# A tenth Strassen pair in the input projection: two merge-gate tiles join it, and the keys' pair moves to its end

## The chip, the cores and the metric

The kernel runs on one core of one Trainium2 chip. The time is what one execution takes on the device, in microseconds; the median of three runs stands for a kernel. A core has five engines that run side by side and wait for each other by semaphores: TensorE (PE, matmuls), VectorE (DVE), ScalarE (ACT), GpSimd (POOL) and SyncE (SP, which here issues the loads). PE writes to PSUM, in banks of 512 fp32 columns; DVE and ACT move results from there to SBUF.

## The reference

One residual block with two token mixers and a SwiGLU, for 512 tokens of width 1024. What matters here is the combined input projection (h, the normalized x, times w_in, its columns split by `IN_SPLITS`) and the GLA mixer that runs beside it (4 heads, chunks of 64):

```python
IN_SPLITS = (GLA_QK_W, GLA_QK_W, GLA_V_W, GLA_V_W, GLA_GATE_RANK,
             NSA_Q_W, NSA_KV_W, NSA_KV_W, NSA_KV_W, NSA_KV_W, NSA_KV_W, NSA_KV_W,
             NSA_GATE_W, D_MODEL, D_MODEL)
...
    attn = jnp.where(causal, jnp.einsum('bhncd,bhnsd->bhncs', qe, ke), 0.0)
    o = jnp.einsum('bhncs,bhnse->bhnce', attn, vh)
...
    o = o + jnp.einsum('bhncd,nbhde->bhnce', qe, s_prev)
    o = o * lax.rsqrt(jnp.mean(o * o, axis=-1, keepdims=True) + RMS_EPS) * norm_g.astype(jnp.float32)
...
    return (o * jax.nn.silu(r.astype(jnp.float32))).astype(r.dtype)
```

GLA's output is A, that of the other mixer (NSA: compressed, selected and window attention, 8 heads) is B, and the two meet as sigmoid(gA) * (A @ w_proj_gla) + sigmoid(gB) * (B @ w_proj_nsa). The last two parts of the split, 1024 columns each, are the merge gates gA and gB. The two parts of 128 columns that are keys of the selected and the window branch are "the keys" below.

## The kernel before, in words

Everything is transposed: a tile is 128 output columns (on the partitions) by 512 tokens. Tiles of the input projection are numbered; `T_GK`, `T_GQ` are GLA's keys and queries, `T_R` its output gate, `T_NQ` NSA's queries, `T_KV` the compressed branch's two inputs and, from `T_KV + 2`, the keys, `T_MA` and `T_MB` the merge gates. Every big fp32 matmul is done as three fp32r products (`three`, L243, L248, L249): high by high, low by high and high by low part. So a weight tile needs a cast (`whi`, ACT L78) and a difference (`wlo`, DVE L85, or an accumulating DMA from POOL).

A **plain** tile takes 8 blocks x 3 matmuls of 512 columns. A **pair** is two tiles computed together by Strassen's scheme in Winograd's form (`EPAIRS`, `eproduct`): 7 products, in the order a11, s2, s3, s1, a22, s4, a12 (`USE`), each of 4 x 3 matmuls of 256 columns. Each product has its weight form: sums of blocks of the two tiles (`esums`, `esum_s1`, `esum_s4`, on DVE) that are split into high and low (`eform`: L415 cast on ACT, L351 difference on DVE, or L418 on ACT and a DMA L420 on POOL). The results go out half by half: a11 by an ACT copy (L490), s2, s3, s1, a22 and s4 by DVE adds (L487), a12 by an ACT copy (L506). A pair has two PSUM banks, and successive pairs take them in opposite order (`ebank`). Where a form lies is fixed by `eplace`: the a22 form of every pair but the last lies in the places tagged `kst` + "s" or "w" (`eks`, `ekw`), that of the last in `e1`, `e2` (`fe`); s4 and a12 forms are called `feq`. Where the results go is fixed by `early_dest`; the keys' tiles go into `kst` + "s"/"w" (`ksts`, `kstw`). The pair's sum `ex` lies in the place tagged `causal`, into which later the attention's mask is set (POOL memset and DMA, L890, L891).

Stages: projection of the token-major part (to about 76 us); then the stage of the pairs, in which GLA runs beside them (to about 229 us); then the compressed branch, attention and the rest. In the second stage `weave` mixes two lists: the products of the pairs and the remaining plain tiles (`Pieces`, `qa`) with the 19 steps of GLA (`gla_attn`, `gla_prep`, `gla_state`, `gla_out`, `gla_end` for four heads). `gla_out` squares its output on ACT (L726, four), forms the inverse root (DVE L287, POOL L288, `grs`) and scales (ACT L731, four); `gla_end` transposes (PE L739), multiplies (DVE L741) and splits (`gh` L273, `gl` L274). The order on each engine is then set by a scheduler that goes by its own estimates; on the chip each engine runs its list in that order.

The plain tiles come through a stream, `st`, that makes each tile's cast and difference one tile ahead. During the pairs this is held back (`st.limit`). At position 18 (`st.reset`) the weights' ring is opened anew: that tile's raw is fetched beforehand, but its cast can only come after the tile ahead has been handed out. Positions 16 to 19 are MA0 to MA3, 20 and 21 the compressed branch's KV0 and KV1. A merge-gate tile ends with a tanh on ACT (`merge_gate`, L771).

## Time and profile before

| | us |
|---|---|
| median of 3 runs (838.72 to 840.14) | 839.0 |
| the profiled execution | 838.92 |
| its span | 837.1 |
| TensorE busy | 823.3 |
| VectorE busy | 634.6 |
| ScalarE busy | 523.0 |
| GpSimd busy | 144.8 |

A row of the timeline has the start in us, the duration, engine, line, operation, output and inputs; in brackets how long the engine had been idle and what released it. A matmul's duration there is modelled and overlaps the next one, so what it costs in a stream is read from the distance between starts. A row of the groups (by line) has the count, the busy time, the mean in ns, and the idle time ahead with its releasers. A row of waits has the waiting engine and tile, the engine, tile and line waited for, the sum in us, how often, and the longest. A row of windows has, for a stretch, its length, then busy us and number of instructions of PE, weight loads, DVE, ACT and POOL, then the granted clock, the DMAs' share and GB/s.

### The profile page before, as it was taken

The page shows a single profiled execution, that of the slowest core. Times are in us where ns is not written, and L with a number is a line of the kernel's source. Part 1 is how long each engine was busy: PE and PEld are TensorE (multiplying, and loading weights), DVE is VectorE, ACT ScalarE, POOL GpSimd, SP SyncE. Part 2 cuts the span into 40 slices and gives each one's busy share as a digit, 9 for nine tenths or more (in the row PEclk, how much of TensorE's full clock was granted, in tenths as well). Part 3 has the DMA queues.
Part 4 walks back from the last instruction along what each step waited for, and adds up shares of the span by engine and source line. Part 5 has one row for each costly group of instructions (what it writes and reads, how often), then busy time and mean ns, then how long its engine had stood idle before and what let it go on. Part 6 is the DMA issues. An engine that isn't in the chain of part 4 may idle for free.

```text
span 837.1 us, 14656 instructions
## 1 busy us (share of the span) xinstructions
PE 823.3 (98%) x5561; PEld 751.2 (90%) x5561; DVE 634.6 (76%) x1205; ACT 523.0 (62%) x967; POOL 144.8 (17%) x174
## 2 busy tenths in 40 slices
PE   9999999999999999999999999999999999999995
PEld 8998899998787887888888999999999999889995
DVE  7765897883477878777666478998888778839986
ACT  6557767773544988887635587766665667445441
POOL 0101022230040000100000265111211110001353
PEclk9999999999999999999999999999999999999998
DMA  8434465762252444454327758778878883325333
GB/s 288 107 106 110 116 124 125 167 146 79 76 184 51 105 122 101 101 120 108 76 76 274 229 141 237 144 208 235 187 194 196 200 177 87 99 67 177 88 102 101
DMA packets 41238, 117.84 MB, mean 141 GB/s; under 512 B 4716, under 2 KB 7036, under 8 KB 41040
## 3 DMA queue, kind: packets, MB, share of 16 engines
q1 hardware_dynamic: 27952, 82.49, 31.3%
q0 software_dynamic: 12496, 33.88, 21.8%
q8 instruction: 43, 0.70, 0.4%
q10 hardware_dynamic: 720, 0.54, 0.2%
q14 instruction: 27, 0.22, 0.1%
HBM read 102.21 MB, written 4.19 MB: 127 GB/s over the span
## 4 chain that ended last, share of the span: by engine, by line
PE 90%; DVE 4%; ACT 4%; issue 1%; DMA 1%; POOL 0%; SPq 0%; DVEq 0%; ACTq 0%
PE ps_mm L243 13%; PE ps_mm L248 13%; PE ps_mm L249 13%; PE ps_sc L243 5%; PE ps_sc L249 5%; PE ps_sc L248 5%; PE ps_acc L243 4%; PE ps_acc L248 4%; PE ps_acc L249 4%; PE ps_tp L568 2%; PE ps_tp L249 2%; PE ps_tp L248 2%; PE ps_tp L243 2%; PE ps_sc L568 2%; PE ps_tp L1132 2%; PE ps_acc L568 1%
## 5 line engine op out<-in xcount | busy, mean ns | idle before, releaser
L78 ACT CAST whi<-wraw 128x1024 fp32r<-128x1024 f32 (+2 forms) x62 | 60.1, 973 | 67.3 <-PE ps_mm L248 25.5
L243 PE MATMUL ps_mm<-hT_hi,whi 128*128 128x512 f32 (+1 forms) x260 | 100.8, 388 | 0.2 <-ACT whi L78 0.2
L249 PE MATMUL ps_mm<-hT_hi,wlo 128*128 128x512 f32 (+1 forms) x260 | 97.4, 375 | 0.0
L248 PE MATMUL ps_mm<-hT_lo,whi 128*128 128x512 f32 (+1 forms) x259 | 96.8, 374 | 0.0
L85 DVE TENSOR_TENSOR wlo<-wraw,whi 128x1024 fp32r<-128x1024 f32 (+2 forms) x47 | 51.4, 1096 | 26.9 <-ACT whi L78 26.9
L243 PEld LDWEIGHTS ps_mm<-hT_hi,whi 128*128 128x128 f32 x260 | 49.0, 189 | 9.7 <-ACT whi L78 0.9
L249 PEld LDWEIGHTS ps_mm<-hT_hi,wlo 128*128 128x128 f32 x260 | 48.9, 188 | 9.3 <-DVE wlo L85 0.3
L248 PEld LDWEIGHTS ps_mm<-hT_lo,whi 128*128 128x128 f32 x259 | 48.8, 189 | 7.1
L1455 ACT CAST d_two<-s 128x1024 fp32r<-128x1024 f32 x26 | 27.0, 1044 | 30.5 <-PE ps_mm L249 15.0
L274 DVE TENSOR_TENSOR pl<-ps_tp,ph 128x512 fp32r<-128x512 f32 (+1 forms) x64 | 31.2, 490 | 19.1 <-ACT ph L273 18.6
L1093 ACT ACTIVATE p<-p,mx 128x512 f32<-128x512 f32 (+1 forms) x64 | 35.8, 561 | 6.7 <-DVE mx L1091 6.5
L1462 DVE TENSOR_TENSOR d_two<-s,d_two 128x1024 fp32r<-128x1024 f32 x25 | 30.6, 1224 | 11.2 <-ACT d_two L1455 10.9
L82 POOL DMA_DIRECT2D wlo<-wraw x15 | 12.8, 851 | 148.3 <-ACT wlo L81 80.6
L1091 DVE CUSTOM_DVE_ANT_0 p<-ps_sc,causal 128x512 f32<-128x512 f32 (+1 forms) x64 | 29.2, 486 | 6.5 <-PE ps_sc L1084 6.2
L273 ACT CAST ph<-ps_tp 128x512 fp32r<-128x512 f32 (+1 forms) x64 | 26.4, 414 | 4.0 <-PE ps_tp L1132 3.5
L1828 POOL TENSOR_TENSOR y<-y,us 128x256 f32<-128x256 f32 x12 | 15.2, 1293 | 72.3 <-DVE us L1825 72.2
L1132 PE MATMUL ps_tp<-ident,p 128*128 128x128 f32 x160 | 27.7, 272 | 0.0
L1132 PEld LDWEIGHTS ps_tp<-ident,p 128*128 128x128 f32 x160 | 20.7, 140 | 7.2 <-ACT pc L1022 0.4
L1439 POOL DMA_DIRECT2D wlo<-in_w_gate x13 | 11.5, 884 | 76.8 <-ACT wlo L1437 76.7
L1455 ACT CAST c_two<-s 128x1024 fp32r<-128x1024 f32 x12 | 12.5, 1045 | 18.8 <-PE ps_mm L249 7.0
L243 PE MATMUL ps_mm<-hT_hi,d_two 128*128 128x256 f32 x80 | 22.4, 281 | 0.0
L249 PE MATMUL ps_mm<-hT_hi,d_two 128*128 128x256 f32 x80 | 22.3, 279 | 0.0
(821 smaller groups left out, 3223.8 us busy)
## 6 DMA issues: line engine op xcount, KB each, us to landing
wraw<-in_w_t SPq DMA_DIRECT2D x36, 512.0 KB, 3.8
wraw<-in_w_gate SPq DMA_DIRECT2D x21, 512.0 KB, 4.4
rw<-in_w_up SPq DMA_DIRECT2D x19, 512.0 KB, 8.3
wlo<-wraw POOLq DMA_DIRECT2D x15, 512.0 KB, 4.5
wlo<-in_w_gate POOLq DMA_DIRECT2D x13, 512.0 KB, 8.6
w_uu<-in_w_up POOLq DMA_DIRECT2D x19, 256.0 KB, 8.7
wraw<-in_w_tok SPq DMA_DIRECT2D x11, 440.0 KB, 3.5
wraw<-in_w_proj SPq DMA_DIRECT2D x8, 512.0 KB, 3.5
```

Source lines behind the costliest of these rows:

```text
L78: self.cast = self.nc.scalar.copy(hi[:, :cols], raw[:, :cols])
L85: self.nc.vector.tensor_tensor(out=lo[:, :cols], in0=raw[:, :cols], in1=hi[:, :cols].bitcast(F32), op=OP.subtract)
L243: pe.matmul(o, wh, xh, start=start, stop=False, skip_group_check=True)
L248: pe.matmul(o[:, c], wh, xl[:, c], start=False, stop=False, skip_group_check=True)
L249: return pe.matmul(o, wl, xh, start=False, stop=stop, skip_group_check=True)
L274: dve.tensor_tensor(out=lo, in0=src, in1=hi.bitcast(F32), op=OP.subtract)
L568: pe.matmul(o, x[:, k, t], y[:, w], start=(k == 0 and m == 0), stop=(k == KD - 1 and m == 2))
L1091: dve.tensor_tensor_reduce(out=o, in0=s, in1=causal[:, S - n:S], scale=-1.0, scalar=-NEG, op0=OP.add, op1=OP.min, accum_out=mx[:, i:i + 1])
L1093: act.activation(out=o, in_=o, func=AF.Exp, scale=-1.0, bias=mx[:, i:i + 1], accum_out=z[:, i:i + 1])
L1132: pe.transpose(tp[:, i * 128:(i + 1) * 128], p[:, OFF[i] + k * 128:OFF[i] + (k + 1) * 128], ident)
L1455: act.copy(hi, t)
L1462: dve.tensor_tensor(out=lo, in0=t, in1=hi.bitcast(F32), op=OP.subtract)
```

## The change

The list of pairs has a tenth entry: MA0 and MA1 (`T_MA`), between the two later output-gate pairs; the query pairs stand together; the keys' pair is the last. So `with_gla` loses two tiles and the weave 8 fills of two. MA0's and MA1's results go to `two0` and `two1` in SBUF, and two tanh behind the weave read them from there. Space for this: the squares of the first stage go to base tags, the triangle mask to the tag `th`, there is one `at` instead of two, and `bl[2]`, `bl[3]` share the places `two0`, `two1`.

```diff
-    with_gla = [("h", n) for n in (T_GK, T_GQ, T_GK + 2, T_GQ + 2)] + [("h", T_MA + n) for n in range(4)]
+    with_gla = [("h", n) for n in (T_GK, T_GQ, T_GK + 2, T_GQ + 2)] + [("h", T_MA + n) for n in (2, 3)]
...
-            sq = acc_x if k == 0 else xin.tile([128, S], F32, tag="sqx", bufs=2, name="sqx")
+            sq = acc_x if k == 0 else base.tile([128, S], F32, tag=("b1", "b5")[k % 2], name="sqx")
...
-    EPAIRS += [(n, n + 1) for n in (T_R, T_R + 2, T_NQ, T_R + 4, T_NQ + 2, T_KV + 2, T_R + 6)]
+    EPAIRS += [(n, n + 1) for n in (T_R, T_R + 2, T_NQ, T_NQ + 2, T_R + 4, T_MA, T_R + 6, T_KV + 2)]
...
     def early_dest(n):
+        if n >= T_MA:
+            ta[n - T_MA] = mid.tile([128, S], F32, tag="two%d" % (n - T_MA), name="two%d" % (n - T_MA))
+            return ta[n - T_MA]
...
-    triu = param("triu", [128, 128], gt)
+    triu = gt.tile([128, S], F32, tag="th", name="triu")[:, 0:128]
+    pool.dma_start(triu, I["triu"])
...
-    ats = []
-    for i in range(2):
-        t = gt.tile([128, NT, 128], F32, name="at%d" % i)
-        pool.memset(t, 0.0)
-        ats.append(t)
+    at = gt.tile([128, NT, 128], F32, name="at")
+    pool.memset(at, 0.0)
...
-    weave(main + [lambda: qa.fill(2)] * 16, steps)
+    weave(main + [lambda: qa.fill(2)] * 8, steps)
+    tas[0] = mid.tile([128, 2, S], F32, tag="gh0", name="ta0")
+    for i in range(2):
+        ta[i] = merge_gate(T_MA + i, tas[0][:, i, :], ta[i])
...
-            bl[j] = mid2.tile([128, S], F32R, name="bl%d" % j)
+            bl[j] = (mid2.tile([128, S], F32R, name="bl%d" % j) if j < 2 else
+                     mid.tile([128, S], F32R, tag="two%d" % (j - 2), name="bl%d" % j))
```

`st.limit` and `st.reset` stay at 14 and 18. Position 18 of the stream was MA2 and is KV0 now. What that does to the engines' lists is shown at three places; a row is line, operation, output, inputs, size and what it waits for.

**First, DVE where the eighth pair's results of s1, a22 and s4 are added.** Before, this is the keys' pair:

```order
L351 TENSOR_TENSOR wlo<-wraw,whi 128x512 [waits PE_49,Activation_49]
L487 TENSOR_TENSOR kstw<-ps_mm,eus 128x256 [waits DMASW5_49,DMASW3_49,DMASW6_49,DMASW0_49,PE_49]
L351 TENSOR_TENSOR wlo<-ex,whi 128x512 [waits DMASW5_49,Activation_49]
L487 TENSOR_TENSOR kstw<-ps_mm,eus 128x256
L351 TENSOR_TENSOR wlo<-wraw,whi 128x512 [waits Activation_49]
L351 TENSOR_TENSOR ex<-wraw,ex 128x512 [waits DVE_49]
L487 TENSOR_TENSOR ksts<-ps_mm,eus 128x256 [waits PE_49]
```

In the change the eighth pair is MA0 and MA1 (an output-gate pair and the keys' pair follow):

```order
L351 TENSOR_TENSOR ex<-wraw 128x512 [waits DVE_49]
L487 TENSOR_TENSOR two_2064<-ps_mm,eus 128x256 [waits PE_49]
L438 TENSOR_TENSOR wraw<-wraw,ex 128x512 [waits DVE_49,Activation_49]
L351 TENSOR_TENSOR wlo<-ex,whi 128x512 [waits DMASW5_49,Activation_49]
L487 TENSOR_TENSOR two_2064<-ps_mm,eus 128x256 [waits PE_49]
L351 TENSOR_TENSOR wlo<-wraw,whi 128x512
L487 TENSOR_TENSOR two_2063<-ps_mm,eus 128x256 [waits PE_49]
```

The first add waited for four DMAs' and PE's use of its place; the add into `two` waits for its product alone.

**Second, ACT and POOL at the third head's output.** ACT before, from that head's squares to the copy of the last pair's a12 result (`sr`), behind which come the plain tiles' casts and tanh:

```order
L726 ACTIVATE go,gssq<-ps_acc 128x256 [waits PE_49] x4
L731 ACTIVATE go<-ps_acc,grs 128x256 [waits Activation_49,Pool_49]
L731 ACTIVATE go<-ps_acc,grs 128x256 [waits Activation_49]
L731 ACTIVATE go<-ps_acc,grs 128x256
L731 ACTIVATE go<-ps_acc,grs 128x256 [waits Activation_49]
L506 COPY sr<-ps_mm 128x256 [waits DVE_49,PE_49]
L764 ACTIVATE th<-sr 128x512 [waits DVE_49,Activation_49]
```

ACT in the change, where `sr` is the result of the pair ahead of the last one, and the last one's forms (`feq`) stand around it:

```order
L726 ACTIVATE go,gssq<-ps_acc 128x256 [waits PE_49] x2
L415 CAST feq_2316<-ex 128x512 [waits DVE_49,Activation_49]
L726 ACTIVATE go,gssq<-ps_acc 128x256 [waits PE_49] x2
L731 ACTIVATE go<-ps_acc,grs 128x256 [waits Activation_49,Pool_49]
L731 ACTIVATE go<-ps_acc,grs 128x256 [waits Activation_49]
L731 ACTIVATE go<-ps_acc,grs 128x256
L731 ACTIVATE go<-ps_acc,grs 128x256 [waits Activation_49]
L506 COPY sr<-ps_mm 128x256 [waits PE_49]
L415 CAST feq_2310<-wraw 128x512
```

POOL in the change; before, the memset, the DMA of `feq` and that of the mask stand in the pair ahead of that output:

```order
L893 MEMSET causal 128x512 [waits DVE_49]
L894 DMA causal<-in_tril_neg 128x128 [waits Pool_49]
L288 TENSOR_TENSOR grs<-grs,mhalf 128x4 [waits DVE_49]
L420 DMA feq_2311<-in_w_t 128x512 [waits DMASW3_49,PE_49,Activation_49]
L288 TENSOR_TENSOR grs<-grs,mhalf 128x4 [waits DVE_49]
```

The copy of `sr` stands behind the scalings in both; in the change the last pair's products follow it on PE instead of MA0 and MA1, and the mask's memset and DMA stand right ahead of the power that the scalings wait for.

**Third, PE and ACT at the end of the stage,** where the last merge-gate tile MA3 ends and KV0 begins. PE before:

```order
L739 MATMUL ps_tp<-ident,go 128x128 [waits PE_49]
L739 MATMUL ps_tp<-ident,go 128x128 x3
L243 MATMUL ps_mm<-hT_hi,whi 128x512
L248 MATMUL ps_mm<-hT_lo,whi 128x512
L249 MATMUL ps_mm<-hT_hi,wlo 128x512 [waits DVE_49]
```

PE in the change, where the third matmul is KV1's first and the fourth is KV0's again, followed by ACT from MA3's tanh on:

```order
L739 MATMUL ps_tp<-ident,go 128x128 [waits PE_49]
L739 MATMUL ps_tp<-ident,go 128x128 x3
L243 MATMUL ps_mm<-hT_hi,whi 128x512 [waits Activation_49]
L248 MATMUL ps_mm<-hT_lo,whi 128x512
L243 MATMUL ps_mm<-hT_hi,whi 128x512 [waits Activation_49]
L249 MATMUL ps_mm<-hT_hi,wlo 128x512 [waits DVE_49]
```
```order
L771 ACTIVATE ta_2493<-ps_mm 128x512 [waits PE_49]
L78 CAST whi<-wraw 128x1024 [waits DMAHW4_49]
L273 CAST gh<-sr 128x512 [waits DVE_49]
L78 CAST whi<-wraw 128x1024 [waits DMAHW5_49,DMASW4_49]
L273 CAST gh<-sr 128x512 [waits DVE_49]
```

Both tiles' casts now stand behind MA3's tanh, with one split of `gh` between them, where before KV0's first matmul waited for nothing.

More of the change, by code (lines that the diff above doesn't have):

```diff
@@ L687, in gla_attn @@
         q3, qk, ku, dec = gst[h]
-        at = ats[h % 2]
         ps = bank("tp")
@@ L716, in gla_out @@
         q3, qk, ku, dec, kut, ss = gst[h]
-        at = ats[h % 2]
         ps = [bank("acc"), bank("acc")]
```

## The prediction

> **What bounds the kernel now.** I read the page first: the busy shares and the chain of work that ended last.
>
> ```profile
> span 837.1 us, 14656 instructions
> PE 823.3 (98%) x5561; PEld 751.2 (90%) x5561; DVE 634.6 (76%) x1205; ACT 523.0 (62%) x967; POOL 144.8 (17%) x174
> ...
> PE 90%; DVE 4%; ACT 4%; issue 1%; DMA 1%; POOL 0%; SPq 0%; DVEq 0%; ACTq 0%
> ```
>
> PE is the bound nearly everywhere, so the change is worth the PE columns that it removes, plus the PE waits that it removes, less those that it adds. Next I asked for PE's waits between 76 and 230 us, which is the stretch that the change reorders.
>
> ```profile
> PE ps_mm L243 <- DVE kstw L487: 0.5, 1, 0.5
> PE ps_mm L243 <- DVE qst L487: 0.2, 1, 0.2
> PE ps_mm L243 <- ACT whi L78: 0.2, 1, 0.2
> ```
>
> There are three waits, each met once, and together they list under one microsecond. So what is there to win is small, and one new wait of a microsecond weighs as much as the columns saved.
>
> **1. Columns.** Two plain tiles are 2 x 24 matmuls of 512 columns. The pair that replaces them is 7 products x 12 matmuls of 256. From PE's timeline:
>
> ```profile
> 98.99 0.39 PE L248 MATMUL ps_mm<-hT_lo,whi 128*128 128x512 f32 x1
> ...
> 100.15 0.28 PE L243 MATMUL ps_mm<-hT_hi,whi 128*128 128x256 f32 x1
> ```
> ```profile
> 101.57 0.28 PE L243 MATMUL ps_mm<-et2gh,whi 128*128 128x256 f32 x1
> ...
> 101.92 0.28 PE L243 MATMUL ps_mm<-et2gh,whi 128*128 128x256 f32 x1
> ```
>
> The first column is the start, the second a modelled duration; what a matmul costs in a stream is the distance between starts. Five of 512 lie between 98.99 and 100.15, so 0.232 us each; three of 256 between 101.57 and 101.92, so 0.1167 us each. 48 x 0.232 = 11.14, 84 x 0.1167 = 9.80: **-1.34 us**. The half-wide matmul costs half, with nothing on top for its weight load.
>
> The Trainium skill, page "TensorE: Matmul & The Clock Gate", section "Back-to-back issue gap", says otherwise: in a sustained stream 128 columns take about 81 ns and 512 about 131, so a matmul's price falls far less than its width. On a line between the two, 256 columns would take some 98 ns (an estimate from that page), and the pair would cost 84 x 0.098 - 48 x 0.131 = +1.9 us where the rows give -1.34. The trace does not agree: its two widths stand at 1 to 2.
>
> **2. The wait on kstw.** This is the s4 product of the keys' pair.
>
> ```profile
> 181.68 0.38 PE L243 MATMUL ps_mm<-hT_hi,feq 128*128 128x256 f32 x1 [0.55 <-DVE kstw L487]
> 181.90 0.28 PE L248 MATMUL ps_mm<-hT_lo,feq 128*128 128x256 f32 x1
> ...
> 182.58 0.28 PE L248 MATMUL ps_mm<-hT_lo,feq 128*128 128x256 f32 x1
> ```
>
> The product accumulates where the pair's s1 result lies, and so waits for the add that moves that result into `kstw`. But this place still holds the pair's own a22 form (`ekw`), so the add waits until PE has done the a22 product, and PE then stands until the add is through. With the keys' pair last, its a22 form lies in `e1`/`e2`, and the eighth pair, now MA0 and MA1, writes to `two0`/`two1`, which nobody reads. The wait goes: 0.55 idle, and 0.22 to the next start instead of 0.11: **-0.65**. If it stayed, 0.
>
> **3. The wait on qst.**
>
> ```profile
> 145.00 0.28 PE L249 MATMUL ps_mm<-hT_hi,feq 128*128 128x256 f32 x1
> 145.50 0.39 PE L243 MATMUL ps_mm<-hT_hi,feq 128*128 128x256 f32 x1 [0.22 <-DVE qst L487]
> ```
>
> 0.50 between starts instead of 0.12: the a12 product of the first query pair waits for the add of its a22 result. In the changed order this add stands on DVE ahead of the `wlo` difference and the masked copy that it stood behind: **-0.38**, or 0 if DVE is late anyway.
>
> **4. The wait at the reset.** Position 18 of the stream is the tile whose raw is fetched but whose cast is not made ahead. Before, that is MA2.
>
> ```profile
> 212.26 1.02 PE L707 MATMUL ps_sc<-tok,gkut 128*128 128x256 f32 x4
> 212.46 0.60 ACT L771 ACTIVATE ta<-ps_mm 128x512 f32<-128x512 f32 x1 [1.18 <-PE ps_mm L249]
> ...
> 212.95 1.98 ACT L78 CAST whi<-wraw 128x1024 fp32r<-128x1024 f32 x2
> 213.12 1.03 PE L723 MATMUL ps_acc<-tok,at 128*128 128x256 f32 x4
> ...
> 214.04 0.50 PE L243 MATMUL ps_mm<-hT_hi,whi 128*128 128x512 f32 x1
> ...
> 214.38 0.40 PE L248 MATMUL ps_mm<-hT_lo,whi 128*128 128x512 f32 x1
> ...
> 214.99 0.51 PE L243 MATMUL ps_mm<-hT_hi,whi 128*128 128x512 f32 x1 [0.21 <-ACT whi L78]
> ```
>
> MA1 ends at 212.26 (call it T). The casts stand on ACT behind its tanh, and the first matmul of MA2 starts at T + 1.78. But eight GLA matmuls (L707, L723) fill 212.26 to 213.98, so only 0.06 is lost ahead of 214.04, then 0.34 - 0.23 = 0.11 and 0.61 - 0.23 = 0.38: **-0.55** when it goes.
>
> **5. New wait B: the same reset, now at KV0.** `with_gla` is two tiles shorter, so position 18 is now the first compress tile. What covers PE between the last merge-gate tile and KV0 is less:
>
> ```profile
> 228.40 1.03 PE L739 MATMUL ps_tp<-ident,go 128*128 128x128 f32 x8
> 229.19 0.48 PE L243 MATMUL ps_mm<-hT_hi,whi 128*128 128x512 f32 x1
> ```
> ```profile
> 228.45 1.06 ACT L78 CAST whi<-wraw 128x1024 fp32r<-128x1024 f32 x1
> ...
> 229.88 1.23 ACT L273 CAST gh<-sr 128x512 fp32r<-128x512 f32 x2
> ```
>
> Eight transposes, 0.79 us; before, KV0 follows them at once, since its cast had been made. After, ACT's order is tanh, KV0's cast, one split of `gh`, KV1's cast; so KV0 starts at T + 1.78 instead of T + 0.79: +0.99. Then PE's order has two matmuls of KV0 (0.34 + 0.23 by part 4) and, third, the first of KV1, which would stand at T + 2.35. KV1's cast waits for KV0's (from T + 0.69, 0.95 by the two starts in part 4) and for the split (1.23 / 2 = 0.61), ends 1.05 later at T + 3.3: +0.95. Everything of KV0 that could have run meanwhile is queued behind that matmul. **+1.95**; at the least 0.99 (only the first half binds), at the most 2.2 (a difference on DVE, L85, is late as well).
>
> **6. New wait A: the s2 product of the last pair.** Pairs take their two banks in alternating order, so the second product (s2) of the keys' pair writes the bank that the last result (a12) of the pair ahead is copied from, by ACT at L506. Before, two plain tiles came next there, and these needed the bank later.
>
> ```profile
> 194.51 1.02 PE L723 MATMUL ps_acc<-tok,at 128*128 128x256 f32 x4
> ...
> 197.35 0.48 PE L243 MATMUL ps_mm<-hT_hi,feq 128*128 128x256 f32 x1
> ```
> ```profile
> 198.31 0.17 DVE L287 TENSOR_SCALAR grs<-gssq 128x4 f32<-128x4 f32 x1 [3.17 <-ACT go L726]
> 198.57 1.03 POOL L288 TENSOR_TENSOR grs<-grs,mhalf 128x4 f32<-128x4 f32 x1 [10.78 <-DVE grs L287]
> 199.64 1.57 ACT L731 ACTIVATE go<-ps_acc,grs 128x256 f32<-128x256 f32 x4 [1.43 <-POOL grs L288]
> 201.08 0.39 ACT L506 COPY sr<-ps_mm 128x256 f32<-128x256 f32 x1
> ```
> ```profile
> 185.41 0.53 POOL L890 MEMSET causal<- 128x512 f32 x1 [6.62 <-DVE feq L351]
> 186.37 0.86 POOL L420 DMA_DIRECT2D feq<-in_w_t  x1 [0.43 <-ACT feq L418]
> 186.90 0.89 POOL L891 DMA_DIRECT2D causal<-in_tril_neg  x1
> ```
>
> Call the start of the third head's output P (194.51). PE does it in 2.84 (to 197.35), then a12 and the next a11 (24 x 0.1167 = 2.80) and one two-pass matmul (0.22): s2 is wanted at P + 5.86. The copy stands on ACT behind four squares, POOL's power and four scalings; at the old pace it ends at P + 6.57 + 0.39 = P + 6.96, which is 1.1 late. But on POOL the power now also stands behind the mask's memset and its DMA. The memset waits for the last pair's s4 difference on DVE (`feq`), which by the order comes behind the second square, at an estimated P + 3.35; with 0.53 and 0.89 the power starts at P + 4.77 and the copy ends at P + 7.8 (1.03 + 1.44 + 0.39 and gaps), 1.9 late. If the DMA holds POOL only for the 0.53 between 186.37 and 186.90, it is 1.5 late. Between these two: **+1.7**, ends 1.1 and 1.9. Behind s2 on PE stand the rest of the pair and everything later, so nothing fills the gap.
>
> **7. At nothing.** The squares' other places and the mask's tag free space and lie in the token stage, whose PE order is unchanged; one memset less is off the path. One `at` instead of two: the masked copy of head h + 1 must follow the output of head h, which PE's order has already. The two tanh of the pair read SBUF and have until the merge. Its three low parts come by accumulating DMAs from POOL, 0.86 each in the row at 186.37, on an engine that is 17% busy.
>
> **Sum.** -1.34 - 0.65 - 0.38 - 0.55 + 1.95 + 1.7 = +0.73. The profiled execution took 838.92 (its span 837.1 and 1.8 around), 0.08 below the median of 839.0: 838.92 + 0.73 + 0.08 = **839.7**.
>
> **A spread that no order tells.** 256 columns take 0.1167 at 101.57, but six of them from 181.90 to 182.58 take 0.113, 3% less. The matmuls run at one or the other pace for long stretches, and a wait can flip them. Of some 100 us reordered, if half changed pace: +-1.5, an estimate.
>
> **Rivals.**
> - **The waits A and B are covered** (PE comes later to both places, by waits elsewhere that take no more time in sum). Then -2.92: 836.1; with A at 1.1 alone, 837.2. For it: PE's present waits are tiny although the order is as tight in many places. Against: in both places the copy and the cast are queued behind something that is itself later than PE's need, by the rows above.
> - **DVE becomes the bound** between 170 and 190 us; this ends slower. A pair costs DVE eight 512-wide sums or differences and five adds of results, less the two `wlo` of plain tiles.
>
> ```profile
> L351 DVE TENSOR_TENSOR ex<-wraw,ex 128x512 f32<-128x512 f32 x8 | 5.5, 685 | 0.0
> L487 DVE TENSOR_TENSOR eus<-ps_mm,eus 128x256 f32<-128x256 f32 x16 | 6.8, 423 | 4.9 <-PE ps_mm L249 4.8
> L85 DVE TENSOR_TENSOR wlo<-wraw,whi 128x1024 fp32r<-128x1024 f32 x5 | 6.0, 1224 | 6.2 <-ACT whi L78 6.2
> ```
> ```profile
> 170.00:180.00 10.00, 10.00 (x91) 10.00 (x90) 7.51 (x18) 8.11 (x18) 3.51 (x4) 1.00 0.69 168
> 180.00:190.00 10.00, 9.45 (x79) 8.92 (x77) 8.95 (x16) 5.60 (x11) 1.95 (x3) 1.00 0.73 162
> ```
>
>   8 x 0.685 + 5 x 0.423 - 2 x 1.224 = +5.1 us, where the third busy column (DVE) leaves 20 - 16.46 = 3.5 idle. From the point where that idle time is used up it costs 1.6 at least, 5.1 if none of it can be used; I take 2.3, near the lower end, since DVE has idled there only in front of PE's results: 842.0. Against: work spreads over the 20 us of two pairs, and PE waits for DVE only twice now.
> - **A half-wide matmul costs more than half.** The pair breaks even at 11.14 / 84 = 0.133 us; at 0.15 it is 12.6 - 11.14 = +1.46 where the sum has -1.34, so 842.5. The rows at 101.57 and 181.90 speak against it. The Trainium skill's page of part 1 has such a rule.
> - That the change doesn't do what it says is excluded by the order: 84 matmuls stand where 48 stood.
>
> **How the numbers follow.** A change under 0.2% (1.7 us) can't be told from none here. The forecast has 0.6 (by its spread 0.42 same, 0.05 faster, 0.13 slower); covered waits 0.18 (0.16 faster, 0.02 same); DVE 0.19 (0.16 slower, 0.03 same); half-width 0.03, slower. Faster 0.21, same 0.47, slower 0.32. With A and B at their bounds the sum is -0.8 to +1.2, and +2.2 if the waits of parts 2 and 3 stay; the pace adds 1.5 either way. The range takes this in, and with it the rivals but for their tails: 836.9 to 842.3.
>
> **What would show it.** Right: in the changed profile the row of waits has no `kstw` and no `qst`, but an ACT `sr` L506 of 1.1 to 1.9 us at the last pair's s2 and an ACT `whi` twice, about 1 us each, at KV0; MA2's start without a wait. Wrong: PE waits for DVE in 150 to 200 us (the DVE rival), no wait on L506 (part 6), KV0 starting 0.8 us behind the last merge-gate matmul (part 5), or starts of 256 columns above 0.125 us in the new pair.

## The result, and the profile after

The changed kernel takes 843.55 us (median of 5 runs, 843.01 to 845.73) where the kernel before takes 839.1: a ratio of 1.0055, with a 95% interval of 1.0045 to 1.0066. The prediction said 839.7 with a range of 836.9 to 842.3, so the time lies outside, and it is slower where no change was the likeliest. The profiled execution of the changed kernel is the slowest of the five, 845.73 (span 843.9, and 1.8 around it). Of all runs below one was slow: one of e5's eleven took 1164.89 us at a granted clock of 0.654, and e5's ratio leaves it out.

From the page of the changed kernel, the lines that answer to those shown of before:

```profile
span 843.9 us, 14750 instructions
...
PE 824.2 (98%) x5597; PEld 752.3 (89%) x5597; DVE 638.7 (76%) x1216; ACT 527.7 (63%) x977; POOL 146.2 (17%) x176
...
PE 84%; DVE 5%; ACT 3%; DMA 3%; issue 2%; POOL 1%; SPq 0%; ACTq 0%; POOLq 0%; DVEq 0%
```

PE is idle for 843.9 - 824.2 = 19.7 us where it was 837.1 - 823.3 = 13.8, and the DMAs' share of the chain went from 1 to 3%. So most of the loss is waiting, and the rows of PE's waits between 76 and 246 us say on whom:

```profile
PE ps_sc L708 <- ACT gs L710: 1.9, 1, 1.9
PE ps_mm L243 <- ACT whi L78: 1.5, 2, 0.7
PE ps_mm L243 <- ACT sr L506: 1.4, 1, 1.4
PE ps_mm L243 <- DVE two L487: 0.9, 1, 0.9
```

The second and third were forecast (parts 5 and 6). The first and the last were not, and a fifth wait comes later, at 291.65:

```profile
285.70 0.86 POOL L82 DMA_DIRECT2D wlo<-wraw  x1 [11.09 <-ACT wlo L81]
...
291.65 0.50 PE L249 MATMUL ps_mm<-ga,wlo 128*128 128x512 f32 x1 [0.82 <-DMA wlo<-wraw]
```

To compare kernels I use one stretch of PE's timeline: from the 415th matmul (in the first pairs, where all kernels are still alike) to the first matmul of the first GLA projection tile (`ga`), below "the stretch". It is 82.99 to 240.17 before, 157.2 us, and 83.10 to 246.07 after, 163.0: +5.8 in the profiled execution. What follows it, up to PE's last matmul, is longer by 1.4 (588.4 and 589.8), of which the wait at 291.65 is 1.0 between starts.

**Wait A as forecast.** POOL, ACT and PE at the third head's output, which starts at 198.68 (P):

```profile
198.68 0.59 PE L723 MATMUL ps_acc<-tok,at 128*128 128x256 f32 x2
```
```profile
201.94 0.53 POOL L893 MEMSET causal<- 128x512 f32 x1 [9.44 <-DVE feq L351]
202.76 0.57 POOL L894 DMA_DIRECT2D causal<-in_tril_neg  x1 [0.30 <-POOL causal L893]
203.35 1.05 POOL L288 TENSOR_TENSOR grs<-grs,mhalf 128x4 f32<-128x4 f32 x1
```
```profile
204.43 1.57 ACT L731 ACTIVATE go<-ps_acc,grs 128x256 f32<-128x256 f32 x4 [2.06 <-POOL grs L288]
205.88 0.39 ACT L506 COPY sr<-ps_mm 128x256 f32<-128x256 f32 x1
```
```profile
204.53 0.39 PE L692 MATMUL ps_tp<-gqk 128*128 128x128 f32 x2
206.32 0.39 PE L243 MATMUL ps_mm<-et2gh,whi 128*128 128x256 f32 x1 [1.40 <-ACT sr L506]
```

The memset starts at P + 3.26 (forecast 3.35), the power at P + 4.67 (4.77), and s2 starts 1.57 later than the matmul ahead of it explains; with 0.11 on the next start that is 1.68, forecast 1.7.

**Wait B as forecast.** ACT and PE at the end of the stage, where MA3 ends at 232.26 (T):

```profile
232.26 1.03 PE L739 MATMUL ps_tp<-ident,go 128*128 128x128 f32 x8
232.46 0.60 ACT L771 ACTIVATE ta<-ps_mm 128x512 f32<-128x512 f32 x1 [0.71 <-PE ps_mm L249]
...
232.95 1.04 ACT L78 CAST whi<-wraw 128x1024 fp32r<-128x1024 f32 x1
233.88 0.62 ACT L273 CAST gh<-sr 128x512 fp32r<-128x512 f32 x1
234.04 0.50 PE L243 MATMUL ps_mm<-hT_hi,whi 128*128 128x512 f32 x1 [0.75 <-ACT whi L78]
...
234.41 1.05 ACT L78 CAST whi<-wraw 128x1024 fp32r<-128x1024 f32 x1
...
235.51 0.50 PE L243 MATMUL ps_mm<-hT_hi,whi 128*128 128x512 f32 x1 [0.73 <-ACT whi L78]
```

KV0 starts at T + 1.78 (forecast T + 1.78) and KV1 at T + 3.25 (T + 3.3): in starts 0.91 + 0.11 and 0.90 + 0.11 lost, 1.95 net of the 0.08 that KV0's start cost before.

**The waits that were not forecast** are of one kind: a cast on ACT waits for its load, and what stands behind it comes late. There are two such casts, and each has its own load. ACT, DVE, PE and SP's queue, in order of time:

```profile
174.23 10.15 SPq L390 DMA_DIRECT2D wraw<-in_w_t  x2
...
180.14 0.62 ACT L415 CAST fe<-wraw 128x512 fp32r<-128x512 f32 x1 [2.36 <-DMA wraw<-in_w_t]
...
182.36 0.69 DVE L351 TENSOR_TENSOR wlo<-ex,whi 128x512 fp32r<-128x512 f32 x1 [1.78 <-ACT whi L415]
...
182.97 0.42 DVE L487 TENSOR_TENSOR two<-ps_mm,eus 128x256 f32<-128x256 f32 x1
...
183.30 0.68 DVE L351 TENSOR_TENSOR wlo<-wraw,whi 128x512 fp32r<-128x512 f32 x1
183.44 0.38 PE L243 MATMUL ps_mm<-hT_hi,feq 128*128 128x256 f32 x1 [0.88 <-DVE two L487]
```
```profile
184.05 0.33 SPq L390 DMA_DIRECT2D wraw<-in_w_t  x1
...
190.19 0.62 ACT L415 CAST whi<-wraw 128x512 fp32r<-128x512 f32 x1 [1.33 <-DMA wraw<-in_w_t]
...
191.25 0.35 ACT L710 COPY gs<-ps_sc 128x256 f32<-128x256 f32 x1
...
191.65 0.70 PE L708 MATMUL ps_sc<-tok,gkut 128*128 128x256 f32 x2 [1.89 <-ACT gs L710]
```

The first raw of the keys' pair is issued at 174.23 and lands some 5.9 us later. The scheduler had put the cast that needs it (`fe`, the last pair's a22 form, wanted by PE only 31 us later) ahead of the ninth pair's casts on ACT; so ACT idles 2.36, the casts behind it come late, DVE's difference waits for them 1.78, and the add into `two` stands behind that. That is the wait on `two` (call it D). D follows ACT's idle time ahead of that cast from trace to trace, and is always 1.3 us less: 2.73 of idle time and 1.4 of D in e10, 2.36 and 1.05 here, 1.95 and 0.61 in e11, 1.84 and 0.52 in e3, 1.75 and 0.43 in e4, and no wait on `two` with 1.43 in e2 and 1.12 in e6.

The difference at 183.30 is the last reader of the place that the second raw of the keys' pair goes to, so this raw is issued at 184.05. It lands 6.0 us later; its cast waits for it on ACT, and behind that cast stands the copy of the third head's first state (`gs`), for which PE stands (C). C does not follow D: it is 1.9 to 2.1 in all six traces that leave both casts and the copy where the change has them, in e6 too, where D is none and the raw is issued 2.4 us earlier:

```profile
181.66 0.33 SPq L390 DMA_DIRECT2D wraw<-in_w_t  x1
```
```profile
187.67 0.62 ACT L415 CAST whi<-wraw 128x512 fp32r<-128x512 f32 x1 [1.19 <-DMA wraw<-in_w_t]
```

What comes right behind C is the granted clock, the third figure from the end in the windows:

```profile
188.96:192.37 3.41, 1.52 (x10) 1.27 (x10) 1.17 (x3) 1.41 (x3) 1.01 (x2) 1.00 0.91 228
192.38:195.78 3.40, 3.40 (x18) 3.40 (x17) 2.19 (x4) 0.00 (x0) 0.12 (x1) 0.50 0.69 105
195.80:199.20 3.40, 3.40 (x30) 3.35 (x29) 2.96 (x6) 1.75 (x3) 0.00 (x0) 1.00 0.00 0
```

For 3.4 us PE has half its clock, 256 columns take 0.21 instead of 0.115, and 1.6 us more are lost. So in the profiled execution the stretch adds up as -1.34 (columns), -0.49 (`qst`), -0.55 (the old reset), +0.33 (the wait on `two`, 1.05 + 0.10, for that on `kstw`, 0.71 + 0.11), +1.68 (A), +1.95 (B), +2.15 (C), +1.6 (half clock) and some 0.9 of smaller waits in the last three pairs: +6.2, against 5.8 measured.

### The profile page after: what moved, and what is told of

Same layout as the page of the kernel before. It is cut to its first block, busy times and chain, and to the rows that moved or that the text cites. A ratio compares the mean times of both kernels' runs of the same rounds, so it can differ in the third digit from the quotient of the medians.

```text
span 843.9 us, 14750 instructions
## 1 busy us (share of the span) xinstructions
PE 824.2 (98%) x5597; PEld 752.3 (89%) x5597; DVE 638.7 (76%) x1216; ACT 527.7 (63%) x977; POOL 146.2 (17%) x176
## 4 chain that ended last, share of the span: by engine, by line
PE 84%; DVE 5%; ACT 3%; DMA 3%; issue 2%; POOL 1%; SPq 0%; ACTq 0%; POOLq 0%; DVEq 0%
PE ps_mm L243 12%; PE ps_mm L249 12%; PE ps_mm L248 12%; PE ps_sc L243 4%; PE ps_sc L249 4%; PE ps_sc L248 4%; PE ps_acc L243 3%; PE ps_acc L248 3%; PE ps_acc L249 3%; PE ps_tp L571 2%; PE ps_tp L249 2%; PE ps_tp L248 2%; PE ps_tp L243 2%; PE ps_sc L571 2%; PE ps_tp L1135 2%
## 5 line engine op out<-in xcount | busy, mean ns | idle before, releaser
L243 PE MATMUL ps_mm<-hT_hi,whi 128*128 128x512 f32 (+1 forms) x248 | 94.5, 381 | 1.5 <-ACT whi L78 1.5
L78 ACT CAST whi<-wraw 128x1024 fp32r<-128x1024 f32 (+2 forms) x60 | 58.3, 973 | 60.1 <-PE ps_mm L248 18.2
L249 PE MATMUL ps_mm<-hT_hi,wlo 128*128 128x512 f32 (+1 forms) x248 | 92.3, 372 | 0.0
L248 PE MATMUL ps_mm<-hT_lo,whi 128*128 128x512 f32 (+2 forms) x247 | 91.7, 372 | 0.0
L85 DVE TENSOR_TENSOR wlo<-wraw,whi 128x1024 fp32r<-128x1024 f32 (+2 forms) x45 | 49.1, 1090 | 21.4 <-ACT whi L78 21.3
L243 PEld LDWEIGHTS ps_mm<-hT_hi,whi 128*128 128x128 f32 x248 | 46.7, 188 | 10.3 <-ACT whi L78 2.2
L249 PEld LDWEIGHTS ps_mm<-hT_hi,wlo 128*128 128x128 f32 x248 | 46.6, 188 | 8.6 <-DVE wlo L85 0.3
L248 PEld LDWEIGHTS ps_mm<-hT_lo,whi 128*128 128x128 f32 x247 | 46.5, 188 | 6.6
L243 PE MATMUL ps_mm<-hT_hi,feq 128*128 128x256 f32 x80 | 23.3, 292 | 0.9 <-DVE two L487 0.9
L415 ACT CAST whi<-wraw 128x512 fp32r<-128x512 f32 x26 | 16.0, 622 | 11.3 <-PE ps_mm L248 7.7
```

What stands on the lines that cost most here:

```text
L78: self.cast = self.nc.scalar.copy(hi[:, :cols], raw[:, :cols])
L85: self.nc.vector.tensor_tensor(out=lo[:, :cols], in0=raw[:, :cols], in1=hi[:, :cols].bitcast(F32), op=OP.subtract)
L243: pe.matmul(o, wh, xh, start=start, stop=False, skip_group_check=True)
L248: pe.matmul(o[:, c], wh, xl[:, c], start=False, stop=False, skip_group_check=True)
L249: return pe.matmul(o, wl, xh, start=False, stop=stop, skip_group_check=True)
```

## The experiments

All edits are to the changed kernel unless said otherwise. Most single runs lie within some 1.5 us of their kernel's median, but e4, e6, e9, e10 and e12 each have one that is 2.7 to 9.2 us above it; and the part behind the stretch, up to PE's last matmul, takes 588.4 to 591.4 us in the traces. So the verdict on a wait rests on its row in the trace, which is one execution, and the verdict on a kernel on its runs.

**e1: hold the `fe` cast.**

```diff
-        with tc.issue_after(stk["plain"].ins) if (u, a) == (1, "s4") else nullcontext():
+        hold = stk["plain"] if (u, a) == (1, "s4") else out_of[u - 1, "a11"] if (u, a) == (NU - 1, "a22") else None
+        with tc.issue_after(hold.ins) if hold else nullcontext():
             act.copy(hi, src)
...
+            with tc.issue_after(hold.ins) if hold else nullcontext():
+                act.activation(out=lo, in_=src, func=AF.Copy, scale=-1.0)
```

> The last pair's a22 form (cast and negated copy, `fe`) is held on ACT behind the copy of the ninth pair's a11 result; nothing else is changed. Theory (a late raw): ACT sat idle 2.36 us ahead of this cast for the raw's DMA, the ninth pair's casts queued behind it, DVE's difference waited for those, and the add into `two` stood behind that difference. Then ACT's wait goes, PE's wait on `two` (0.88, 1.05 between starts) goes, and the time falls by about 1.0 from 843.55 to 842.5; the wait on `gs` stays. Rival (DVE is simply full there): the add is still late, PE waits for `two` 0.5 us or more, time within 0.4 of 843.55.

842.92 us, ratio to before 1.0044 (1.0032 to 1.0056). From PE's waits, and SP's queue, of e1:

```profile
PE ps_mm L243 <- ACT sr L507: 1.5, 1, 1.5
PE ps_mm L243 <- ACT whi L78: 1.5, 2, 0.7
PE ps_sc L709 <- ACT gs L711: 0.2, 1, 0.2
```
```profile
181.73 0.33 SPq L390 DMA_DIRECT2D wraw<-in_w_t  x1
```

The wait on `two` is gone, and so it is in all five traces in which the `fe` cast is held. Since it is missing without the hold too, in e2 and e6, one trace alone would not show the cause; that D goes with ACT's idle time ahead of the cast does. Against the expectation, nearly all of the wait on `gs` is gone too. The second raw is issued at 181.73 instead of 184.05, but that alone is not why, since e6 issues it as early and keeps C. It also lands sooner, after 4.5 us. In the five traces with the hold (e1, e5, e9, e12, e13) this raw takes 4.5 to 5.6 us, in the seven others 5.9 to 6.1. In those the low part of `fe`, which POOL fetches behind that cast, is under way at the same time (issued at 181.60 in the change, landing after 4.1); whether the two transfers slow each other was not tried by itself.

The stretch is 158.1, 4.9 shorter (1.0 of D, 1.7 of C, 1.6 of half clock, 0.6 not told apart). The median fell by 0.6 only. The two traces overstate the edit, since that of the change is its slowest execution of five and that of e1 the fastest of five, and D is not of one size, as shown above; what else the runs keep stays open.

**e2: `gs` of the third head copied by DVE.**

```diff
-                act.copy(ss[:, 0, :], ps[:, 0:256])
+                (dve.tensor_copy if h == 2 else act.copy)(ss[:, 0, :], ps[:, 0:256])
```

> The copy of the third head's first state (`gs`) is made by DVE instead of ACT; nothing else is changed. Theory (a late raw): on ACT this copy stood behind the cast of the keys' pair's a11 form, which waited for its raw's DMA; DVE was idle there. Then PE's wait on `gs` (1.89, 2.05 more between starts) goes, with it the half clock of the 3 us behind it, and the time falls by 2 to 3 from 843.55, to about 841.2; the granted clock is 0.996 in every run. Rival (PE is behind its operands there anyway): another wait of about the same length takes its place within the next two products, and the time stays within 0.7 of 843.55.

844.19 us (842.5 to 844.42). In the trace the wait on `gs` fell from 2.05 to 0.54 between starts, PE's clock stayed whole, and the stretch is 158.7. In this trace D is none as well. That the copy's place was the cause is seen from ACT, which starts the cast that had stood ahead of it at 188.28, when PE has already gone on at 188.09. The runs do not show a gain: they are not told apart from the changed kernel's (ratio to before 1.0058, 1.0045 to 1.0071, against 1.0055). So the wait is ACT's line; the gain in time is not shown by this experiment.

**e3: the copy of `sr` by DVE.**

```diff
-                act.copy(d0[:, halves[0]], o)
+                (dve.tensor_copy if u == NU - 2 else act.copy)(d0[:, halves[0]], o)
```

> The a12 result of the pair ahead of the last (`sr`) is copied by DVE instead of ACT; nothing else is changed. Theory (part 6 of the prediction): the s2 product of the last pair waits for this copy, which stood on ACT behind the third head's scalings; DVE copies at once. The wait on `sr` (1.4, 1.57 more between starts) goes: about -1.6, to 841.9. Rival: the next thing late (the cast of the s3 form, or the matmul behind it) takes the place of most of it: -0.5 or less, 843.0 and above.

845.47 us, ratio 1.0071 (1.0058 to 1.0085): no gain. s2 waits no more, but the next product does, for the next copy in the same line of ACT:

```profile
207.13 0.39 ACT L490 COPY eus<-ps_mm 128x256 f32<-128x256 f32 x1
...
207.56 0.39 PE L243 MATMUL ps_mm<-et3gh,whi 128*128 128x256 f32 x1 [1.05 <-ACT eus L490]
```

1.57 between starts became 1.21. The rival holds: what is late is ACT behind the scalings, not one copy.

**e4: the ring opened anew at MA3.**

```diff
-    st.limit, st.reset = 14, 18
+    st.limit, st.reset = 14, 17
...
-    main = sum((pair(u) for u in range(2, NU - 1)), []) + pair(NU - 1, (17, 18))
+    main = sum((pair(u) for u in range(2, NU - 1)), []) + pair(NU - 1, (17,), (1,))
```

> The ring is opened anew at position 17 (MA3) instead of 18 (KV0), as before the change it was at a merge-gate tile; nothing else is changed. Theory (part 5): the two waits of KV0 and KV1 on their casts (0.91 + 0.11 and 0.90 + 0.11 more between starts) go, and MA3 pays what MA2 paid before the change, about 0.55, since GLA's matmuls cover most of it: -1.4, to 842.1. Rival: MA3 has less cover than MA2 had, and pays 1.5 or more: 843.0 and above.

844.13 us (841.66 to 848.66), ratio 1.0064 (1.0042 to 1.0087). In the trace the two waits at KV0 and KV1 (0.91 and 0.90) are gone, and MA3 pays 0.49 and 0.38: 0.9 less. The stretch is 159.7, 3.3 shorter, but 1.6 of that is the half clock, which this trace does not have, and 0.6 a smaller D. The runs scatter too much to show 0.9. (The second part of the edit follows from the first: the stream is made ahead up to position 17 behind the last pair's s2, and no more up to 18 behind its s1.)

**e6 and e10: the low part of a later tile on DVE.** e6 took pa 2, which is the tile ahead of the one that waits; e10 took pa 3.

```diff
-    st.on_dma = set(with_att) | {(x, n) for x in "gu" for n in range(1, NPLAIN)}
+    st.on_dma = set(with_att[1:]) | {(x, n) for x in "gu" for n in range(1, NPLAIN)}
```
```diff
-    st.on_dma = set(with_att) | {(x, n) for x in "gu" for n in range(1, NPLAIN)}
+    st.on_dma = set(with_att) - {("pa", 3)} | {(x, n) for x in "gu" for n in range(1, NPLAIN)}
```

> The changed kernel, with the low part of one later tile (the third GLA projection tile) made by a difference on DVE instead of an accumulating DMA from POOL; nothing else is changed. Theory (a collision after the stage): in the changed kernel this DMA lands 5.9 us after its issue instead of about 4.9, and PE waits 0.8 for it (1.0 between starts), which the kernel before does not. The wait on `wlo` goes, with 1.2 us more on DVE that nobody waits for: -1.0, to 842.6. Rival (the tile would be late on any way, since the stage ahead ends differently): the wait moves to DVE, no gain, within 0.4 of 843.55.

> The changed kernel, with the low part of the fourth GLA projection tile (pa 3) on DVE: e6 had taken the tile ahead of the one that waits. Theory: the DMA on which the instruction fetch falls is gone, no wait of PE on `wlo<-wraw` is left between 240 and 300 us, and the stretch behind the pairs is as long as in the kernel before (588.4 us there, 589.8 in the changed kernel): -0.9, to 842.6. Rival: the wait moves to the next tile with such a DMA, as it did in e6, 0.4 or more.

e6: 844.64 us (ratio 1.0076, 1.0063 to 1.0088); the wait on `wlo` is still there, 0.4. The edit missed its tile. e10: 843.54 us (ratio 1.0059, 1.004 to 1.0077); no wait on `wlo` is left, and the part behind the stretch is 589.2 instead of 589.8 (588.4 before). A wait of 1.0 less is in the trace, and lost in the scatter of the runs.

**e7: eighteen small matmuls in the kernel before.**

```diff
+    ps = bank("sc")
+    for i in range(18):
+        pe.matmul(ps[:, i:i + 1], ident, ident[:, 0:1], start=True, stop=True)
     qa = Pieces(with_gla)
```

> The kernel before, with 18 fp32 matmuls of one column put in ahead of the pairs (36 passes, so 36 matmuls and 36 weight loads more on PE, as many as the change adds; their result is written over). Theory: the DMA of that low part is late in the changed kernel because PE's instruction fetch (one 16 KB transfer on one DMA engine) now falls on it, 8 us earlier in the program than before. Then the kernel before with as many more PE instructions has the wait too: PE waits for `wlo<-wraw` 0.6 to 1.0 us at the third GLA projection tile, and the time is 839 + 1 + the small matmuls' own 2 to 4. Rival (the order of the stage or of POOL's queue is the cause): no wait on `wlo` there.

843.37 us in one run. The trace has two matmuls and two weight loads for each of the eighteen, 72 instructions as the change adds, and they are busy for 4.1 us themselves, so its time is read from the wait and not from the run. The kernel before, with its own order of everything, now has the wait of the changed kernel at the same tile, 6.0 us behind the DMA's issue:

```profile
282.50 0.86 POOL L82 DMA_DIRECT2D wlo<-wraw  x1 [11.11 <-ACT wlo L81]
...
288.55 0.51 PE L249 MATMUL ps_mm<-ga,wlo 128*128 128x512 f32 x1 [0.94 <-DMA wlo<-wraw]
```

The DMAs of those 7 us, in the changed kernel (285 to 292) and, last line, in the kernel before (279 to 286, where no row of the instruction kind stands); the last figure of an issue is us to landing:

```profile
q8 instruction: 1, 0.02, 1.0%
...
wlo<-wraw POOLq DMA_DIRECT2D x1, 512.0 KB, 5.9
```
```profile
wlo<-wraw POOLq DMA_DIRECT2D x1, 512.0 KB, 4.5
```

Queue q8 moves 43 packets of 16 KB in the kernel before, 0.70 MB, which is 63 bytes for each of PE's 2 x 5561 matmuls and weight loads; so I take it for PE's instruction fetch. The change adds 72 PE instructions, and each fetch behind them falls due earlier in the program. One of them now falls on this low part, whose tile has no time to spare. Nine of the traces have a fetch of q8 between this transfer's issue and its landing, which takes 5.5 to 6.1 us in them; the kernel before and e8 have the transfer without a fetch, and it takes 4.5. That PE comes to this tile later is not the cause: e5 comes to it 0.7 us earlier than the kernel before and waits all the same (0.66). That the fetch itself delays the transfer was not tried by itself; that the count of PE's instructions decides where it falls, e7 shows.

**e8: the kernel before, with only the keys' pair moved to the end.**

```diff
-    EPAIRS += [(n, n + 1) for n in (T_R, T_R + 2, T_NQ, T_R + 4, T_NQ + 2, T_KV + 2, T_R + 6)]
+    EPAIRS += [(n, n + 1) for n in (T_R, T_R + 2, T_NQ, T_R + 4, T_NQ + 2, T_R + 6, T_KV + 2)]
```

> The kernel before, with the keys' pair moved to the end of the list (behind the last output-gate pair) and nothing else of the change. Part 2 of the prediction (the add into `kstw` waits for the place of `ekw`): PE's wait at the s4 product of the eighth pair goes, -0.65. Rival (DVE reaches that add late, behind a difference that waits for an ACT cast): the wait stays at the same place, now on the output-gate pair's add, 0.4 us or more; the last pair's a22 cast waits for its raw on ACT as in the changed kernel. By both the s2 wait on L506 can't come, since two plain tiles still stand behind the eighth pair or the pair behind it; within 1.0 of 838.8.

838.59 us, ratio 0.9995 (0.9987 to 1.0004). The wait at the eighth pair's s4 is gone, as part 2 forecast, but PE waits 0.5 (0.67 between starts) for a square of the second head instead; the stretch is 157.0 for 157.2. So this part of the change alone neither gains nor loses.

**e11: the power ahead of the mask's memset.**

```diff
-    pool.memset(causal, 0.0)
+    with tc.issue_after(stk["pow"].ins):
+        pool.memset(causal, 0.0)
```

> The changed kernel, with the mask's memset and DMA held on POOL behind the third head's power. Part 6 of the prediction: without them the copy of `sr` is 1.1 late instead of 1.7, since the power starts as soon as DVE has formed its input. PE's wait at the last pair's s2 falls by 0.5 to 0.7, from 1.57 more between starts to about 1.0. Rival (the squares and scalings on ACT alone set the copy): the wait stays at 1.4 or more.

845.48 us in one run. The wait at s2 fell from 1.57 to 1.15 between starts (1.4 to 1.0 in the waits): part 6 had 1.7 and 1.1.

**e5, e9, e12, e13: the edits together.** e5 has those of e1, e3 (with the last pair's a11 copy on DVE too), e4 and e6. e9 has pa 3 for pa 2, and the gate of the pair ahead of the last formed behind the last pair's s1. e12 adds e11, makes the last pair's a11 form one product later, and holds that gate and MA2's low part behind the last pair's s1 add. e13 adds to e12:

```diff
+            if n == NU - 1:
+                with tc.issue_after(stk["gs"].ins):
+                    eform(n, "a11", True)
```

and the same hold for `fe`, where `stk["gs"]` is the copy of `gs`; the a11 form is made one more product later (behind s1).

> The changed kernel with five edits together: the last pair's a22 form held (e1), the copies of `sr` and of the last pair's a11 result on DVE (e3, with the copy that took the wait over), the ring opened anew at MA3 (e4), the third GLA projection tile's low part on DVE (e6). Theory: what the change loses are these waits, so they add up: against the changed kernel -1.05 and -1.7 and the half clock (e1's trace), -1.5, -1.4, -1.0, so 843.55 - 6.6 = 837.0, about 1.8 below the kernel before (-1.34 of columns, -0.5 of the add on `qst`). Rival (removing a wait here only moves it to the next operand that is late, as in e3): 839.5 or above.

> As e5, with the low part of the right tile on DVE (pa 3 instead of pa 2), and the gate of the pair ahead of the last (tanh and multiply, `sr`) formed behind the last pair's s1 result instead of ahead of its s2, because in e5 that multiply on DVE held up an add and PE waited 1.0 (1.18 between starts) for it. Theory: both waits go and the rest of e5 stays, 840.4 - 1.1 - 0.8 = 838.5, 0.5 below the kernel before. Rival: another operand is late there by as much, 840 or above.

> As e9, with four more orders set by hand: the mask's memset behind the power (e11), the last pair's a11 form made one product later, the gate of the pair ahead of the last held on DVE behind the last pair's s1 add, and the low part of MA2 made behind that add. In e9's trace PE still lost 0.83 at `gs`, 0.31 and 0.60 at two adds of `eus` that stood behind these. Theory (what is lost is what stands in the wrong order on ACT and DVE): these go for the most part, the stretch of the pairs falls from 156.7 to about 155.3 us (157.2 in the kernel before) and the time to about 838.3, 1.0 below the kernel before. Rival (ACT and DVE have too much work there for any order): the stretch stays at 156.3 or more and the time at 839.4 or above.

> As e12, with the last pair's a11 and a22 forms held on ACT behind the copy of `gs`, so that no cast that waits for a raw stands ahead of it. In e12's trace PE still lost 0.89 at `gs`. Theory (the wait is the cast ahead of it, not ACT's load): the wait on `gs` goes, the stretch of the pairs falls from 155.8 to about 154.9 us (157.2 in the kernel before), the time to about 838.0. Rival (ACT is late there in any order): the wait on `gs` stays at 0.5 or more, or the raw's cast is late for the last pair's a11 product instead; the stretch stays at 155.6 or more.

| | us, median | ratio to before, 95% | stretch | PE's waits that were left in it, between starts |
|---|---|---|---|---|
| e5 | 840.39 | 1.0016 (1.0008 to 1.0025) | 156.5 | 1.18 `eus`, 0.67 `gs`, 0.49 + 0.38 MA3 |
| e9 | 839.66 | 1.0008 (0.9997 to 1.0018) | 156.7 | 0.83 `gs`, 0.31 + 0.60 `eus`, 0.49 + 0.38 |
| e12 | 838.75 | 1.0004 (0.9984 to 1.0024) | 155.8 | 0.89 `gs`, 0.49 + 0.38 |
| e13 | 837.71 | 0.9988 (0.9979 to 0.9997) | 154.6 | 0.27 at the matmul that had waited for `gs`, 0.49 + 0.38 |

(e12's interval is wide because one of its runs took 848.) From e5 on the time falls with each step, though e5 still moved one wait to the next operand and e9's stretch is no shorter than e5's. e13 has all of the change's work, 5597 matmuls, and is below both kernels, 1.4 us under the kernel before and 5.8 under the changed one. These times are of the runs; the traced execution is 839.58, 1.9 above e13's median, and in it PE waits 2.1 between starts for `y`, at 769.22, where the other traces have 1.1 at most. Its PE waits between 76 and 330 us are

```profile
PE ps_mm L243 <- ACT whi L78: 0.5, 2, 0.3
PE ps_sc L1100 <- DVE mx L1108: 0.3, 1, 0.3
PE ps_acc L1164 <- DVE pl L274: 0.2, 1, 0.2
```

So the wait on `gs` was the casts ahead of it, and ACT's load did not set it.

## Why the prediction was wrong

| the prediction's step | forecast | in the trace of the change |
|---|---|---|
| 1 columns | -1.34 | -1.35 by the mean distances between starts in the stretch (84 x 0.1161 for 48 x 0.2312); in the time not told apart |
| 2 wait on `kstw` | -0.65 | the wait stayed, as one on `two`: +0.33 |
| 3 wait on `qst` | -0.38 | gone, with its next start -0.49 |
| 4 old reset | -0.55 | gone |
| 5 wait B | +1.95 | +1.95 |
| 6 wait A | +1.7 | +1.68 |
| sum, "-1.34 - 0.65 - 0.38 - 0.55 + 1.95 + 1.7" | +0.73 | C +2.15, smaller waits +0.9, half clock +1.6 (not in every execution) and +1.0 behind the stretch are missing |

**The step that failed is the sum: it took A and B for the only waits that the change adds.** It follows A and B to what they wait for, but has no term for a cast of a pair's form that waits for its load. Part 7, on what is put at nothing, names the low parts' DMAs and not the raws, so these waits were put at nothing without a reason. D (1.05), C (2.15) and, behind C, the half clock (1.6) are what stands in its place. It was not asked when the load could be issued, nor how long after it the scheduler had put the cast. The trace of before shows part of this: between 100 and 175 us its raws came 3.8 to 5.7 us after their issue, three places hold them, and the cast of `fe` stands 14.4 us behind the issue of its raw (at 160.79), where ACT waits for no DMA:

```profile
175.17 0.62 ACT L415 CAST fe<-wraw 128x512 fp32r<-128x512 f32 x1 [0.45 <-DVE gqk L675]
```

In the change it stands 5.9 us behind the issue. The tenth pair's raw is issued 13.4 us later than that of the ninth had been, at 174.23, while ACT comes to the cast at 177.8 instead of 174.7, only 3.1 us later. How long that load would take could be read from the trace of before only as a range.

**Part 2 was wrong in its cause.** It said that the add into `kstw` waits until PE has read `ekw`. The rows of DVE in the kernel before say that the add was simply next in DVE's line:

```profile
180.60 0.68 DVE L351 TENSOR_TENSOR wlo<-wraw,whi 128x512 fp32r<-128x512 f32 x1
...
181.21 0.42 DVE L487 TENSOR_TENSOR kstw<-ps_mm,eus 128x256 f32<-128x256 f32 x1
```

DVE had no idle time between the two. A wait that stands in an instruction is not yet the wait that held it. In e8, where nothing but the order changed, the wait went; in the change it came back in `two`, through the late cast.

**Part 7 was wrong for what lies behind the stage:** 72 more PE instructions were counted at nothing, and cost 1.0 by e7.

**The rivals.** "DVE becomes the bound" gave 842.0, near the time, and its sign, a wait of PE for DVE between 150 and 200 us, did come (0.88 at 183.44). It is still not what happened: at the one add for which PE waited, DVE had been idle 1.78 us for ACT. Half-wide matmuls cost half here too, in the new pair itself, where six starts lie 0.114 us apart:

```profile
177.79 0.28 PE L243 MATMUL ps_mm<-et1gh,whi 128*128 128x256 f32 x1
...
178.36 0.28 PE L249 MATMUL ps_mm<-et1gh,wlo 128*128 128x256 f32 x1
```

The sign fell on the side of slower because the two waits that were forecast alone ate the saving, and the unforeseen ones had nothing against them.

**The pace** of the matmuls, which the prediction put at up to 1.5 us either way, is in these traces too. Inside the stretch the starts of 256 columns lie 0.1160 us apart on average before, 0.1161 in the change, 0.1160 in e12 and 0.1148 in e13. Over the 883 such matmuls of the changed kernel 0.0012 is about 1 us. So of the 2.6 us by which e13's stretch is shorter than that of the kernel before, and of the 1.2 from e12 to e13, about 1 us can be pace and not order. It is no part of why the prediction failed, since before and the change have the same.

## What to carry to other kernels

On an engine that runs its line in order, a cast that waits for a load is paid by everything behind it: for each such instruction compare the time from the load's issue to the place where the scheduler has put it with what the loads of the trace take, above all where a list gets longer and loads move back by an item. When a wait is removed, look at the next two instructions in the same line first: in e3, e5 and e8 the wait moved on to another operand. The work saved by the change (1.34 us by the prediction's rows) became a gain only with all the edits of e13 to the order. No edit by itself lowered the runs' median clear of their scatter.

## What the runs showed of the hardware

A wait of PE of 1.9 to 2.1 us between starts was followed by 3.4 us at a granted clock of 0.5 in four of the seven traces that have one (the change, e3, e6, e11; not in e4 and e10, nor in e13 behind its wait for `y`), and no wait of 1.7 or less was. The price is 1.6 us, nearly as much as the wait itself.

Where the wait falls decides which. In every trace the clock changes on a grid of 3.41 us. In the four traces the stretch of the grid ahead of the half clock holds the whole wait, and PE is busy in it for 1.5 to 1.7 us, 43 to 49% (1.52 in the row of 188.96 above). In the three others an edge of the grid cuts the wait, and PE is busy for 1.9 to 2.05 us, 56 to 60%, on the side that has more of it. In e10, the nearest, the wait begins ahead of the edge:

```profile
189.41:192.82 3.41, 1.90 (x14) 1.85 (x15) 1.31 (x4) 1.41 (x3) 0.86 (x1) 1.00 0.84 196
```

The grid of these three is counted back from the end of the program, where the clock falls too. The Trainium skill, "TensorE: Matmul & The Clock Gate", section "What's actually happening", has a clock that halves after at least one idle window of some 3.4 us, by a window that runs freely. The length and the free grid fit the traces; that the window has to be idle does not, since here PE was busy for 43 to 49% of it. What share is the limit, between 49 and 56%, was not tried.

An instruction fetch of 16 KB on a low part's DMA went with 5.9 us from issue to landing instead of 4.5; its place follows the number of PE's instructions, so an edit can cost a microsecond far behind itself: some 100 us behind the new pair in the change, and 220 us behind the small matmuls in e7.
